# Attention: exponentials multiplied unscaled, inverse row sums applied to a head pair's result

## The chip, the cores and the metric

One core of one Trainium2 chip runs the whole program. Its engines are TensorE (PE, matmuls and transposes), VectorE (DVE), ScalarE (ACT), GpSimd (POOL) and SyncE (SP, which here only issues DMAs). The metric is device time of one execution in microseconds. A profiled execution is a further one, from which the trace comes.

## The reference

Two layers work on x of 512 positions by 1024 channels. Each layer is a gated feed-forward block (FFN), a mixer, and another such block. The mixer projects its normalised input into three branches, two of which are attentions with 8 heads of 64 channels. The change is in these. For each head:

```
logits = q . k + bias            # first attention: by distance; second: by forget gates
logits = where(visible, logits, -1e30)
p = softmax(logits)              # exp(logits - max) / sum
out = p @ v
```

The first attention sees its own chunk of 64 positions and eight chunks before it, the second everything up to the own position. The three branches are multiplied by branch weights, gated, added up and projected back.

## The kernel before, in words

Everything is held transposed: channels on the 128 partitions, the 512 positions (`T`) along the free axis. Matmuls of 32-bit numbers are made of three matmuls of high and low parts (`triple`, lines 117 to 122; `mm` at L119, L120 and L121): each operand is split into `hi`, a rounded copy made by ACT, and `lo`, the rest, made by a subtraction. `split_to` (L377 to L379) does this: ACT copies at L378, DVE or POOL subtracts at L379. Weights come in chunks of 512 KB on SP's queue and are split in `wchunk` (ACT at L271, DVE at L273).

Each attention (`attention`) runs over 8 heads and 4 blocks of 128 query positions (`NT` = 4), so 32 steps, two attentions in each of two layers: 128 steps in all, and 16 pairs of heads. A step has three parts, which are issued at different times:

- `logits`: two matmuls (L951, L952) give the scores of 128 queries against the first `n` = 128 to 512 keys in a PSUM bank. DVE adds the bias strip and takes the maximum (L955), ACT takes the exponential and its row sum (L959), DVE inverts the sum (L961), and the exponentials are multiplied by it (L962), on POOL for the first three blocks of a head and on DVE for the last.
- `turn`: PE transposes the scaled exponentials 128 columns at a time (L974), and ACT and DVE split them into high and low (L978, L979).
- `weigh`: for each half of the queries (two blocks), matmuls of v with the turned exponentials (L996, L997). The head's 64 channels come out in one half of the partitions for v's high part and in the other for its low part; ACT moves one half over (L1000), DVE adds (L1001), and `split_to` splits the sum into the pair's block `y` (ACT at L378, POOL at L379, pieces of 64 partitions by 256 columns).

The order is written by hand: `later(delay, ...)` queues a function until a count of PE work (`pe[0]`, in units of one 512-column matmul) has grown by `delay`, and `poll`, called before each triple, runs what is due. `LAG_T` = 24 is the delay from scores to transposes, `LAG_V` = 14 from there to `weigh`. Between the steps a filler feeds PE: projections for the second attention during the first, gates and the first branch's merge (`merge_units`) during the second, 9.5 and 9.0 units a step. The first merge unit runs all queued work of the first attention (`poll(group="a")`) before it uses the four pair blocks `ys`. From the written order the compiler makes the order on each engine; an engine takes its instructions strictly in that order.

Buffers are rings under a tag, and a tile whose ring is full waits for the oldest to be let go: `t2` has three buffers of 512 columns (exponentials, squares, and others), `t1` two (scores, pieces of the output, gates), `b` 17 blocks of 1024 columns (turned q and k, pair results and others), and four PSUM banks have the tag `mm` (scores, transposes, pieces of the output).

The bias strips of a head are loaded on SP's queue one head ahead; in the first attention POOL clears a corner of them (L926), in the second it masks each with four additions (L937). POOL's queue also copies x to DRAM ahead of a mixer (L1119), and scales half of the blocks of q and k (L839).

Of the kernel before, what the change touches and what calls it, by code (L numbers as in the profile page):

```python
# [15 lines left out]
F32 = mybir.dt.float32  # L16
F32R = mybir.dt.float32r
I32 = mybir.dt.int32
AF = mybir.ActivationFunctionType
ALU = mybir.AluOpType  # L20
AX = mybir.AxisListType

P = 128
T = 512
# [6 lines left out]
HD = 64  # L31
NT = T // P
# [8 lines left out]
def encoder_kernel(tc, xT, c, w_ada, b_ada, gains, w_gate, w_up, w_down, w_qkv, w_f, w_ubg,  # L41
                   qk_gain, rel, fbias, w_pool, pool_scale, w_branch, w_out, inv_cnt, w_first, out):
    nc = tc.nc
    pools = []

    def open_pool(**kw):
        p = tc.tile_pool(**kw)
        pools.append(p)
        return p.__enter__()
# [4 lines left out]
    dr = open_pool(name="dr", bufs=1, space=bass.MemoryType.DRAM)  # L54
# [3 lines left out]
    NB, NRAW = 17, 2  # L58

    def nm(s):  # L60
        uid[0] += 1
        return f"{s}_{uid[0]}"

    def st(shape, dt, tag, bufs):
        return sb.tile(shape, dt, tag=tag, bufs=bufs, name=nm(tag))
# [4 lines left out]
    def mmt(shape=(P, T)):  # L70
        return ps.tile(list(shape), F32, tag="mm", bufs=4, name=nm("mm"))

    def blk(tag, dt=F32R):
        bufs = {"xv": 4, "v2": 4, "b": NB}[tag]
        return st([P, 2, T], dt, tag, bufs)

    def t1(cols=T):
        return st([P, cols], F32, "t1", 2)

    def t2(cols=T):  # L80
        return st([P, cols], F32, "t2", 3)
# [16 lines left out]
    def later(delay, fn, group=None):  # L98
        t = Task(pe[0] + delay, fn, group)
        tasks.append(t)  # L100
        return t

    def poll(everything=False, group=None):
        if polling[0]:
            return
        polling[0] = True
        while True:
            ready = [t for t in tasks if t.fn is None or everything or t.due <= pe[0]
                     or (group is not None and t.group == group)]
            if not ready:  # L110
                break
            t = min(ready, key=lambda z: z.due)
            tasks.remove(t)
            t.run()
        polling[0] = False
# [56 lines left out]

    x_dram = dr.tile([4, P, 2 * T], F32, name="x_dram")
    fv_dram = [dr.tile([H, FVLEN], F32, name=f"fv_dram{l}") for l in range(L)]

    last = {}

# [199 lines left out]
    def split_to(hi, lo, src, lo_eng=nc.vector):  # L377
        nc.scalar.copy(hi, src)  # L378
        lo_eng.tensor_tensor(lo, src, hi.bitcast(F32), op=ALU.subtract)  # L379
# [502 lines left out]
    def finish_turns(upto=3):  # L882

        for todo in turns:
            while len(todo) >= 4 - upto:
                todo.pop(0)()
# [53 lines left out]
    def attention(qs, ks, vs, strip, ys, filler, budget, group):  # L940


        open_pt = {}

        def logits(h, i, strips):
            p, off = divmod(h, 2)
            (q, ql), k = qs[p], ks[p]
            odd = h % 2
            n = (i + 1) * P
            s = mmt()  # L950
            mm(s[:, :n], q[:, odd, i * P:(i + 1) * P], k[:, odd, :n], start=True, stop=False)  # L951
            mm(s[:, :n], ql[:, odd, i * P:(i + 1) * P], k[:, odd, :n], start=False, stop=True)  # L952
            lg = t1(T)[:, :n]
            mx = st([P, 1], F32, "mx", 4)
            nc.vector.tensor_tensor_reduce(out=lg, in0=s[:, :n], in1=strips[i], scale=-1.0, scalar=BIG,  # L955
                                           op0=ALU.add, op1=ALU.min, accum_out=mx)
            pr = t2(T)[:, :n]
            sm = st([P, 1], F32, "sm", 4)
            nc.scalar.activation(pr, lg, AF.Exp, bias=mx, scale=-1.0, accum_out=sm)  # L959
            rs = st([P, 1], F32, "rs", 4)  # L960
            nc.vector.reciprocal(rs, sm)  # L961
            (nc.vector if i == NT - 1 else nc.gpsimd).tensor_scalar(pr, pr, rs, None, op0=ALU.mult)  # L962
            pe[0] += 0.5 * (i + 1.5)
            later(LAG_T, lambda: turn(h, i, pr), group)

        def turn(h, i, pr):
            half, c = divmod(i, 2)
            nj = 2 * half + 2
            if c == 0:
                open_pt[h] = st([P, 2, nj, 256], F32R, "ptb" if half else "pta", 2 if half else 1)  # L970
            pt = open_pt[h]
            tp = mmt()
            for j in range(i + 1):
                nc.tensor.transpose(tp[:, j * P:(j + 1) * P], pr[:, j * P:(j + 1) * P], ident)  # L974
            tv = tp[:, :(i + 1) * P].rearrange("p (j q) -> p j q", q=P)
            dh = pt[:, 0, :i + 1, c * P:(c + 1) * P]
            dl = pt[:, 1, :i + 1, c * P:(c + 1) * P]
            nc.scalar.copy(dh, tv)  # L978
            nc.vector.tensor_tensor(dl, tv, dh.bitcast(F32), op=ALU.subtract)  # L979
            pe[0] += 0.55 * (i + 1)  # L980
            if c == 1:
                later(LAG_V, lambda: weigh(h, half, pt), group)

        def weigh(h, half, pt):
            p, off = divmod(h, 2)
            rows = slice(off * HD, off * HD + HD)
            other = slice(HD - off * HD, 2 * HD - off * HD)
            if off == 0 and half == 0:
                ys.append(blk("b"))
            y = ys[p]  # L990
            o = mmt((P, HALF))
            nj = 2 * half + 2
            for j in range(nj):
                q0 = P if j == nj - 1 else 0
                v2 = vs[j][:, h, :, :].rearrange("p a d -> p (a d)")
                mm(o[:, q0:], v2, pt[:, 0, j, q0:], start=(j == 0), stop=False)  # L996
                mm(o[:, q0:], v2, pt[:, 1, j, q0:], start=False, stop=(j == nj - 1))  # L997
            cols = slice(half * HALF, (half + 1) * HALF)
            yl = t1(T)[:, :HALF]
            nc.scalar.copy(yl[rows, :], o[other, :])  # L1000
            nc.vector.tensor_tensor(yl[rows, :], o[rows, :], yl[rows, :], op=ALU.add)  # L1001
            split_to(y[rows, 0, cols], y[rows, 1, cols], yl[rows, :], nc.gpsimd)
            pe[0] += 1.0 * nj

        for h in range(H):
            strips = strip(h)
            if group == "c":
                finish_turns(h // 2)
            for i in range(NT):
                logits(h, i, strips)  # L1010
                if i == NT - 1:
                    heads[0] = h + 1
                poll()
                goal = pe[0] + budget
                while filler is not None and pe[0] < goal:
                    if next(filler, "end") == "end":
                        filler = None
                poll()
        if filler is not None:
            for _ in filler:  # L1020
                pass

    LAG_T, LAG_V = 24, 14


    def pool_front(l, g):
# [77 lines left out]
    class Mixer:  # L1104
# [10 lines left out]
        def run(self, nxt):  # L1115
# [19 lines left out]

            lo_share[0] = LO_SHARE
            attention(qa, ka, va, lambda h: strip_a(l, h), ya, fill_a(), FILL_A, "a")
            heads[0] = H

# [23 lines left out]
            def fill_c():  # L1163
                yield from merge_units(l, 0, ya, put_a)

            attention(qc, kc, vc, lambda h: strip_c(l, h), yc, fill_c(), FILL_C, "c")
            finish_turns()
            turns.clear()
# [102 lines left out]
```

## Time and profile before

| | |
|---|---|
| median of 3 runs | 2451.54 us |
| lowest and highest run | 2450.65 and 2452.75 us |
| the profiled execution | 2450.88 us |
| its span, first to last instruction | 2448.9 us |
| mean granted clock of TensorE | 0.998 |
| first layer's attentions in the trace | 460 to 690 us |
| second layer's attentions | 1667 to 1895 us |

In the rows of the profile, "line engine operation out<-in xcount" names a group of instructions by the line of the kernel, and tiles by their names in the program with the numbers left off (a tile made by `t1` or `t2` is called `t`). A wait row "A <- B: total, times, longest" says that A stood idle until B had finished. PEld is PE's loading of weights, which runs beside its matmuls. Matmuls overlap, so the duration of one is longer than the distance to the next.

### The profile page before, as it was taken

To read this page: it belongs to the slowest core of one execution; us is meant where nothing else is said; L and a number is where in the kernel's file an instruction comes from. 1 tells how busy PE (TensorE), PEld (TensorE's weight loads), DVE (VectorE), ACT (ScalarE), POOL (GpSimd) and SP (SyncE) were. 2 spreads that over 40 slices of the span, in tenths; PEclk is the share of its full clock that TensorE was granted. 3 is DMA by queue.
4 is the path that set the end of the run, shared out by engine and by line. 5 is a ranking of instruction groups with operands and counts; after the bars stand their busy time and mean duration, and the time that the engine had idled before them with its cause. 6 is when DMAs were issued, how large, how long until landed. Compare 5 with 4: busy or idle time off the path is not lost. (4 is left out here: it accounts for less than half of the span.)

```text
span 2448.9 us, 34028 instructions
## 1 busy us (share of the span) xinstructions
PE 2396.8 (98%) x12966; PEld 2051.8 (84%) x12966; DVE 1600.5 (65%) x2859; ACT 1110.3 (45%) x1888; POOL 377.3 (15%) x439
## 2 busy tenths in 40 slices
PE   7999999999999999999999999999999999999999
PEld 5798888777888898988898888878777888988888
DVE  8978766677643378787678656477765434765463
ACT  5333345677642353333453334366765333533341
POOL 3000002144532110000000000123354322000000
PEclk9999999999999999999999999999999999999999
DMA  7756543222323426565327423223133234233232
GB/s 284 251 170 209 198 147 113 78 82 88 116 91 103 142 75 240 174 206 198 129 85 243 138 86 121 103 90 96 61 109 99 95 111 139 87 104 112 67 114 78
DMA packets 116279, 320.23 MB, mean 131 GB/s; under 512 B 11122, under 2 KB 13298, under 8 KB 116116
## 3 DMA queue, kind: packets, MB, share of 16 engines
q1 hardware_dynamic: 114962, 313.86, 38.3%
q0 software_dynamic: 1152, 4.19, 0.4%
q8 instruction: 102, 1.67, 0.3%
q14 instruction: 61, 0.50, 0.1%
q10 hardware_dynamic: 2, 0.00, 0.0%
HBM read 311.64 MB, written 6.38 MB: 130 GB/s over the span
## 5 line engine op out<-in xcount | busy, mean ns | idle before, releaser
L271 ACT CAST whi<-raw 128x1024 fp32r<-128x1024 f32 (+1 forms) x325 | 338.2, 1044 | 595.1 <-PE mm L120 289.2
L273 DVE TENSOR_TENSOR wlo<-raw,whi 128x1024 fp32r<-128x1024 f32 x317 | 392.2, 1240 | 197.4 <-ACT whi L271 194.2
L121 PE MATMUL mm<-hhi,wlo 128*128 128x512 f32 x744 | 289.8, 390 | 0.7 <-DVE wlo L273 0.4
L119 PE MATMUL mm<-hhi,whi 128*128 128x512 f32 x744 | 290.2, 390 | 0.0
L120 PE MATMUL mm<-hlo,whi 128*128 128x512 f32 x744 | 290.0, 390 | 0.0
L119 PE MATMUL acc<-b,whi 128*128 128x512 f32 (+1 forms) x704 | 264.1, 376 | 1.7 <-ACT b L378 1.7
L121 PE MATMUL acc<-b,wlo 128*128 128x512 f32 (+1 forms) x704 | 262.1, 374 | 3.5 <-DVE wlo L273 3.5
L120 PE MATMUL acc<-b,whi 128*128 128x512 f32 (+1 forms) x704 | 262.4, 373 | 0.0
L197 DVE CUSTOM_DVE_ANT_0 v<-v,b,badac 128x1024 f32<-128x1024 f32 x144 | 188.3, 1316 | 60.9 <-DMA v<-in_w_ada_dram 60.7
L119 PE MATMUL acc<-hhi,whi 128*128 128x512 f32 x480 | 190.7, 399 | 1.7 <-ACT hhi L738 1.7
L121 PE MATMUL acc<-hhi,wlo 128*128 128x512 f32 x480 | 188.9, 394 | 0.0
L120 PE MATMUL acc<-hlo,whi 128*128 128x512 f32 x480 | 188.5, 393 | 0.2 <-DVE hlo L741 0.2
L121 PEld LDWEIGHTS mm<-hhi,wlo 128*128 128x128 f32 x744 | 139.7, 188 | 30.9 <-DVE wlo L273 1.6
L119 PEld LDWEIGHTS mm<-hhi,whi 128*128 128x128 f32 x744 | 140.0, 188 | 27.9
L120 PEld LDWEIGHTS mm<-hlo,whi 128*128 128x128 f32 x744 | 139.7, 188 | 27.4
L121 PEld LDWEIGHTS acc<-b,wlo 128*128 128x128 f32 x704 | 133.8, 190 | 27.2 <-DVE wlo L273 4.6
L119 PEld LDWEIGHTS acc<-b,whi 128*128 128x128 f32 x704 | 133.3, 190 | 23.8 <-ACT b L378 2.6
L120 PEld LDWEIGHTS acc<-b,whi 128*128 128x128 f32 x704 | 133.3, 189 | 23.2 <-DVE b L379 0.9
L119 PE MATMUL acc<-whi,hhi 128*128 128x512 f32 x336 | 137.7, 411 | 4.4 <-ACT t L828 3.7
L120 PE MATMUL mm<-b,whi 128*128 128x512 f32 (+1 forms) x384 | 135.8, 354 | 0.0
L119 PE MATMUL mm<-b,whi 128*128 128x512 f32 (+1 forms) x384 | 135.8, 354 | 0.0
L121 PE MATMUL mm<-b,wlo 128*128 128x512 f32 (+1 forms) x384 | 135.6, 354 | 0.0
(300 smaller groups left out, 5598.3 us busy)
## 6 DMA issues: line engine op xcount, KB each, us to landing
v<-in_w_ada_dram SPq DMA_DIRECT2D x144, 512.0 KB, 4.4
raw<-in_w_down_dram SPq DMA_DIRECT2D x88, 512.0 KB, 3.5
raw<-in_w_up_dram SPq DMA_DIRECT2D x82, 512.0 KB, 3.4
b<-in_w_gate_dram SPq DMA_DIRECT2D x76, 512.0 KB, 5.3
raw<-in_w_ubg_dram SPq DMA_DIRECT2D x56, 512.0 KB, 3.3
raw<-in_w_qkv_dram SPq DMA_DIRECT2D x42, 512.0 KB, 3.7
raw<-in_w_branch_dram SPq DMA_DIRECT2D x24, 512.0 KB, 3.6
raw<-in_w_out_dram SPq DMA_DIRECT2D x16, 512.0 KB, 3.3
```

Of the source, the lines that this page charges most:

```text
L119: mm(o, lh, rh, start=start, stop=False, skip_group_check=onto)
L120: mm(o, lh, rl, start=False, stop=False, skip_group_check=onto)
L121: mm(o, ll, rh, start=False, stop=stop, skip_group_check=onto)
L197: dot = nc.vector.tensor_tensor_reduce(out=raw, in0=raw, in1=silc[0], scale=1.0, scalar=badac[:, l, j, d:d + 1], op0=ALU.mult, op1=ALU.add ...
L271: nc.scalar.copy(hi, raw)
L273: lo_eng.tensor_tensor(lo, raw, hi.bitcast(F32), op=ALU.subtract)
```

## The change

The exponentials are turned and multiplied as they are. The row sums of a pair of heads are collected in one tile of 128 by 8 (partition: query in the block; column: head and block). After the pair's last exponential DVE inverts all of it, and a DMA on POOL's queue writes it to DRAM as two rows of 512. `weigh` adds its pieces into a row block of the `b` ring and no longer splits them. Eight units of PE work after the pair's last piece, `norm_rows` has two DMAs on POOL's queue spread the two rows of inverse sums over 64 partitions each (`rb`, from the `t2` ring); DVE multiplies the whole row block by it, and `split_to` splits it into the pair's block with ACT and DVE.

```diff
+    inv_dram = {(g, p): dr.tile([2, T], F32, name=f"inv_dram_{g}{p}") for g in "ac" for p in range(4)}
...
             pr = t2(T)[:, :n]
-            sm = st([P, 1], F32, "sm", 4)
-            nc.scalar.activation(pr, lg, AF.Exp, bias=mx, scale=-1.0, accum_out=sm)
-            rs = st([P, 1], F32, "rs", 4)
-            nc.vector.reciprocal(rs, sm)
-            (nc.vector if i == NT - 1 else nc.gpsimd).tensor_scalar(pr, pr, rs, None, op0=ALU.mult)
+            if odd == 0 and i == 0:
+                sums[p] = st([P, 2 * NT], F32, "sm", 3)
+            nc.scalar.activation(pr, lg, AF.Exp, bias=mx, scale=-1.0,
+                                 accum_out=sums[p][:, odd * NT + i:odd * NT + i + 1])
+            if odd and i == NT - 1:
+                rs = st([P, 2 * NT], F32, "rs", 2)
+                nc.vector.reciprocal(rs, sums[p])
+                nc.gpsimd.dma_start(inv_dram[group, p].rearrange("h (i q) -> q (h i)", q=P), rs)
             pe[0] += 0.5 * (i + 1.5)
             later(LAG_T, lambda: turn(h, i, pr), group)
...
             if off == 0 and half == 0:
-                ys.append(blk("b"))
-            y = ys[p]
+                rows_of[p] = st([P, T], F32, "b", NB)
+            y = rows_of[p]
...
             nc.scalar.copy(yl[rows, :], o[other, :])
-            nc.vector.tensor_tensor(yl[rows, :], o[rows, :], yl[rows, :], op=ALU.add)
-            split_to(y[rows, 0, cols], y[rows, 1, cols], yl[rows, :], nc.gpsimd)
+            nc.vector.tensor_tensor(y[rows, cols], o[rows, :], yl[rows, :], op=ALU.add)
             pe[0] += 1.0 * nj
+            if off and half:
+                later(LAG_N, lambda: norm_rows(p), group)
+
+        def norm_rows(p):
+            rb = t2(T)
+            for z in range(2):
+                nc.gpsimd.dma_start(rb[z * HD:(z + 1) * HD, :], inv_dram[group, p][z:z + 1, :].broadcast_to([HD, T]))
+            y = blk("b")
+            ys.append(y)
+            full = rows_of[p]
+            nc.vector.tensor_tensor(full, full, rb, op=ALU.mult)
+            split_to(y[:, 0, :], y[:, 1, :], full)
...
-    LAG_T, LAG_V = 24, 14
+    LAG_T, LAG_V, LAG_N = 24, 14, 8
```

More of the change, by code (lines that the diff above doesn't have):

```diff
@@ L943, in attention @@
         open_pt = {}
+        sums, rows_of = {}, {}
         def logits(h, i, strips):
```

## The prediction

> **What bounds the kernel now.** I read the page's first lines, then the busy time by stretch, then the waits of TensorE (PE), and last the groups of instructions that the diff touches.
>
> ```profile
> span 2448.9 us, 34028 instructions
> ## 1 busy us (share of the span) xinstructions
> PE 2396.8 (98%) x12966; PEld 2051.8 (84%) x12966; DVE 1600.5 (65%) x2859; ACT 1110.3 (45%) x1888; POOL 377.3 (15%) x439
> ```
>
> PE is the bound: 98% of the span. Only its idle time can be won, 52 us in all. The next view says where that is; its columns are PE, PEld (weight loads), VectorE (DVE), ScalarE (ACT), GpSimd (POOL), the granted clock and the DMAs.
>
> ```profile
> 460.00:580.00 120.00, 112.20 (x579) 89.03 (x578) 87.99 (x222) 84.93 (x182) 42.53 (x54) 1.00 0.26 80
> 580.00:690.00 110.00, 105.78 (x568) 86.79 (x567) 70.38 (x190) 69.76 (x168) 59.12 (x83) 0.98 0.34 108
> 1667.00:1780.00 113.00, 106.14 (x551) 84.72 (x550) 82.20 (x205) 80.15 (x172) 41.08 (x50) 1.00 0.27 80
> 1780.00:1895.00 115.00, 108.20 (x578) 86.79 (x577) 74.56 (x205) 72.35 (x176) 60.64 (x85) 1.00 0.34 104
> 720.00:860.00 140.00, 140.00 (x622) 116.06 (x621) 51.27 (x53) 43.69 (x56) 29.34 (x17) 1.00 0.36 121
> ```
>
> The first four rows are the two attentions of each layer, the fifth the stretch behind them, where PE never rests. In attention PE is idle for 7.8, 4.2, 6.9 and 6.8 us: 25.7 us is all that this change can reach. DVE and ACT are at 64 to 74% there, so delays on them do get through. The waits of PE from the first attention to the end of the last (total us, times, longest):
>
> ```profile
> PE mm L974 <- POOL t L962: 6.8, 15, 0.7
> PE mm L951 <- DVE t L1001: 4.6, 6, 1.1
> PE mm L951 <- DVE ptb L979: 3.0, 2, 1.5
> ...
> PE mm L951 <- DVE mx L955: 1.8, 4, 0.7
> PE mm L974 <- DVE ptb L979: 1.7, 4, 0.5
> PE mm L997 <- DVE ptb L979: 1.2, 4, 0.3
> PE mm L974 <- DVE rs L961: 1.0, 2, 0.5
> ```
>
> Two rows are transposes (L974) that wait for the scaled exponentials: 6.8 + 1.0 = 7.8 us, the change's own. The other five, 12.3 us, are PE waiting for DVE: scores that want a PSUM bank back, or the low halves of turned weights.
>
> **Part 1: reciprocal and multiply leave each of 128 steps.**
>
> ```profile
> L961 DVE RECIPROCAL rs<-sm x128: 144/162/166, 465.4 to 1887.2; 128x1 f32<-128x1 f32 x128
> L962 POOL TENSOR_SCALAR t<-t,rs x96: 602/927/1253, 465.7 to 1882.5; 128x128 f32<-128x128 f32 x32, 128x256 f32<-128x256 f32 x32, 128x384 f32<-128x384 f32 x32
> L962 DVE TENSOR_SCALAR t<-t,rs x32: 465/487/781, 473.4 to 1887.4; 128x512 f32<-128x512 f32 x32
> ```
>
> Durations are minimum, median and maximum in ns. DVE loses 128 x 0.162 + 32 x 0.487 = 36.3 us of work, POOL 96 x 0.927 = 89 us. The way from exponential to transpose gets shorter by a reciprocal and a multiply, at least 0.144 + 0.465 = 0.6 us, mostly over 1 us. No single wait was longer than 0.7 us, so nearly all of the 7.8 us goes. The same view says who waited for these lines; the weight loads of the transposes stood longer than PE:
>
> ```profile
>   PEld mm L974: 14.0, 20
> ```
>
> The upper bound is that 14.0 plus the 1.0 behind DVE: 15. I take 8, as PE's own rows are the nearer ones. What is late next is the same transpose behind ACT's exponential, or a bank behind DVE: I give back 2 us (bounds 0 and 8).
>
> And it says what DVE itself stood idle for before L961:
>
> ```profile
>   ACT t L959: 37.6, 66
> ```
>
> So DVE stood 37.6 us, 66 times, in front of the reciprocal until ACT had finished the sum. With 16 reciprocals in place of 128, an eighth of it stays: 33 us of blocked queue go. Everything queued behind it (the low halves at L979, L273's subtractions, the score pass L955) moves up. Of PE's 12.3 us behind DVE I take a third, 4 us; bounds 0 and 12.3.
>
> **Part 2: the split moves from 64 quarter pieces to 16 pairs.**
>
> ```profile
> L378 ACT CAST b<-t x64: 388/405/411, 477.1 to 1893.8; 64x256 fp32r<-64x256 f32 x64
> ...
> L378 ACT CAST v<-xv x8: 619/620/620, 782.7 to 2016.4; 128x512 fp32r<-128x512 f32 x8
> ```
>
> ```profile
> L379 POOL TENSOR_TENSOR b<-t,b x64: 723/737/1750, 477.6 to 1894.2; 64x256 fp32r<-64x256 f32 x64
> ...
> L379 DVE TENSOR_TENSOR v<-xv,v x8: 692/693/693, 783.3 to 2017.0; 128x512 fp32r<-128x512 f32 x8
> ```
>
> ACT loses 64 x 0.405 = 25.9 us and gets 16 x 0.620 = 9.9. POOL loses 64 x 0.737 = 47.2. DVE gets, for each pair, one reciprocal, one multiply and one subtraction of 128x512, both priced by the 0.693 row: 16 x (0.162 + 2 x 0.693) = 24.8 us. Against the 36.3 lost, DVE's work falls by 11.5 us in 458 us of attention. That is inside the 4 us above. The buffer `t` of the output piece is free after the add, no longer after POOL's subtraction; ACT and DVE waited for that, PE did not, so it counts as zero.
>
> **Part 3: three DMAs per pair on POOL's queue, and a multiply that waits for them.** No transfer of this shape is in the trace. The nearest are the copy of x to DRAM from POOL's queue, the strips that SyncE's queue (SP) spreads over the partitions from a row of DRAM, and POOL's waits for those:
>
> ```profile
> L1119 POOL DMA_DIRECT2D x_dram<-xv x8: 573/573/762, 365.9 to 1596.4; - x8
> ```
>
> ```profile
> x_dram<-xv POOLq DMA_DIRECT2D x8, 512.0 KB, 3.2
> strip<-in_rel_dram SPq DMA_DIRECT2D x16, 256.0 KB, 2.7
> ssum<-fv_dram SPq DMA_DIRECT2D x16, 256.0 KB, 3.1
> ```
>
> ```profile
> POOL strip L937 <- DMA strip<-fv_dram: 11.9, 11, 2.1
> ```
>
> POOL is busy 0.573 us with issuing a DMA of 128 rows. The two spreading reads have 64 rows each: 2 x 0.573 = 1.15 us, landing 3.1 us later (a row of DRAM spread over partitions, as theirs is). The write has 128 x 8 = 1024 pieces of 4 bytes, because a column of 128 partitions becomes a row in DRAM. Its issue costs between 0.573 us (by DMA) and 8 x 0.573 = 4.6 us (by piece); I take 4.6 since the number of pieces is what differs, and 3.2 us more to land. POOL then has 16 x (4.6 + 1.15) = 92 us more, or 28 at the lower end, against 89 + 47 = 136 us fewer. POOL is no one's bound.
>
> The Trainium skill, page "DMA: Bandwidth & Descriptors", section "Rules for kernel authors", speaks against the write: a DMA whose last dimension is not contiguous becomes one descriptor per element. By that rule the price by piece, 4.6 us, holds and the sum stays as below; its effect here is rival (c); no row here shows such a write.
>
> Who is queued behind: the write waits for the reciprocal, and POOL's queue (clearing and masking of strips, the scaling of q and k) stands behind it. The reads wait for the write and for one of three `t2` buffers, which the exponentials use as well. The multiply waits on DVE for the reads, and L955, L979, L273 stand behind it. Where the compiler puts the multiply in DVE's order decides. POOL's masking shows how well that goes with DRAM reads: 11 waits, 11.9 us, so 1.1 us each. For 16 pairs that is 17 us of DVE standing, half of the 33 us just freed. At the exchange rate of part 1 (4 us of PE for about 44 us of DVE: 33 + 11.5) it costs 2 us; I take 3, as these come in one piece. Bounds: 0, and the second rival.
>
> **Part 4: the hand-over to the merge.** Inside an attention nobody waits for a pair's result; after the first attention the first merge takes all four. From the timeline, the last exponential of the first attention:
>
> ```profile
> 584.20 0.71 ACT L959 ACTIVATE t<-t,mx 128x512 f32<-128x512 f32 x1
> ```
>
> the copy of the last piece:
>
> ```profile
> 594.00 0.36 ACT L1000 COPY t<-mm 64x256 f32<-64x256 f32 x1 [0.98 <-POOL b L379]
> ```
>
> and PE's use of the result:
>
> ```profile
> 596.32 0.40 PE L119 MATMUL acc<-b,whi 128*128 128x512 f32 x1
> ```
>
> New: row sums at about 585, write landed by 585 + 4.6 + 3.2 = 592.8, reads by 592.8 + 1.15 + 3.1 = 597.1, then 0.693 and 0.620 for the high half: 598.4, 2.1 us late. With the cheap write the reads land at 593.1, and the add behind the copy (594.0 + 0.36, and about as long again) is the last, at 594.8: high half at 596.1, in time. Twice in the program, so 0 to 4 us; I take 1, since the copy's own 0.98 us of waiting goes too. After the second attention four pool projections of 24 matmuls each lie between: nothing.
>
> **Sum**, against the profiled execution's 2450.88 us (span 2448.9 and 2.0 around it): -8 + 2 - 4 + 3 + 1 = -6, so 2444.9. The median of the runs, 2451.54, is 0.66 above that execution: **2445.5 us**.
>
> **Rivals.** (a) *Given back in full.* The transposes come on time, but the scores then meet the bank or DVE they would have met anyway. For it: five of seven rows are DVE's, and a queue in order passes time on. Against: DVE is relieved too. Give-back 6, relief 1: -8 + 6 - 1 + 3 + 1 = +1, so 2452 to 2449 with relief 2 to 4; no change.
>
> (b) *DVE stands in front of the multiply.* If the order puts it at the reads' issue, DVE stands up to 1.15 + 3.1 = 4.2 us for each pair. PE's cover is the four PSUM banks: attention has 32 steps in some 114 us, 3.6 us each, and a step takes two banks or more, so cover is under two steps, less DVE's backlog: about 3 us. It decides from 3 us of standing. Beyond it PE loses up to 16 x (4.2 - 3) = 19 us, less the 6 + 3 won elsewhere: +10, 2461. Against: the 1.1 us above.
>
> (c) *The write blocks POOL in front of the masks*, at 4.6 us of issue or more. A head's masks end with
>
> ```profile
> 655.66 0.46 POOL L937 TENSOR_TENSOR ssum<-ssum,cmask 128x128 f32<-128x128 f32 x1
> ```
>
> and are first used at
>
> ```profile
> 657.21 0.28 DVE L955 CUSTOM_DVE_ANT_0 t<-mm,strip 128x128 f32<-128x128 f32 x1
> ```
>
> 656.1 to 657.2 leaves 1.1 us. With 4.6 us of issue in front they are 3.5 late, at three heads of each second attention; (b)'s cover of 3 us leaves 6 x 0.5 = 3. If the issue is twice as dear, 9.2, they are 8.1 late: 6 x 5.1 = 31 us, less the 6 won, 2476. It decides above about 5 us of issue. The rule of the Trainium skill in part 3, one descriptor per element, is what would bring it about. Against: the scaling that stood in POOL's way is gone.
>
> (d) *No shorter.* The row block and its split block want the `b` ring of 17, which holds up to 16 long-lived blocks in attention; the output pieces then wait. About 2450, and 2455 if the next projections wait.
>
> **How the numbers follow.** Forecast 0.50, its own range 2438 to 2449; (a) 0.26, (b) 0.12, (c) 0.07, (d) 0.05. About 0.2%, 4.9 us, is what a measurement can tell from no change. Below 2446.6: 0.44, all from the forecast. Within: the rest of it 0.06, (a) 0.26, half of (d): 0.35. Above 2456.4: (b), (c) and the other half of (d), 0.21. The low end, 2437, is 15 + 12.3 won, half of it given back; the high end, 2459, takes in (a) and most of (b).
>
> **What would show it.** Right: no PE wait on L962; PE idle in the four stretches down from 25.7 to about 20; DVE's work about 11 us lower; waits of DVE for the spread sums near 1 us each; the write's issue on POOL between 0.6 and 4.6 us. Wrong: PE waits at L951 growing by as much as L974's shrank (a); DVE waits of over 3 us on a DMA with PE idle behind (b); DVE waiting for strips (c); PE's busy time itself changed, which nothing here touches.

## The result, and the profile after

| | before | after |
|---|---|---|
| median of 4 runs each, same chip | 2452.14 us | 2533.37 us |
| lowest and highest | 2450.65, 2454.41 | 2527.49, 2533.92 |
| profiled execution | 2450.88 | 2533.92 |

The ratio is 1.0325, with a 95% interval of 1.0307 to 1.0343: the change makes the kernel 81 us slower. The forecast was 6 us faster, and the range ended at 2459. Two executions among the experiments below, of 4.8 and 13.6 ms, were disturbed and are left out of their medians.

In the changed kernel most lines of the attention have moved. The ones needed below: exponential L962, reciprocal L966, the write to DRAM L967, transposes L979, copy and subtraction of turned weights L983 and L984, weighing L1001 and L1002, add of the halves L1006, the two reads L1014, the multiply L1018, the split's copy L379, the strips' load L932 and mask L938.

The page of the changed kernel, its first lines:

```profile
span 2532.2 us, 33690 instructions
## 1 busy us (share of the span) xinstructions
PE 2416.9 (95%) x12966; PEld 2069.8 (82%) x12966; DVE 1590.1 (63%) x2747; ACT 1092.3 (43%) x1840; POOL 256.7 (10%) x327
```

The span grew by 83.3 us. PE's idle time, span less busy, went from 52.1 to 115.3 us (+63.2), and its busy time from 2396.8 to 2416.9 (+20.1) with the same 12966 matmuls. All other engines do less than before: DVE 10.4 us, ACT 18.0, POOL 120.6. So no engine is the new bound; something makes them wait.

Busy time by stretch of the changed kernel, its four attentions (columns as in the prediction):

```profile
460.00:594.00 134.00, 122.49 (x626) 98.94 (x624) 91.07 (x209) 87.93 (x189) 20.23 (x35) 0.97 0.32 85
594.00:738.00 144.00, 112.79 (x563) 93.08 (x560) 62.53 (x147) 58.19 (x140) 21.50 (x45) 0.89 0.32 85
...
1715.00:1850.00 135.00, 123.12 (x633) 99.44 (x631) 92.41 (x212) 89.22 (x193) 20.51 (x35) 0.97 0.35 85
1850.00:1983.00 133.00, 106.80 (x539) 88.21 (x539) 59.37 (x142) 54.85 (x132) 20.22 (x44) 0.91 0.36 87
```

These stretches take 546 us where they took 458. That +88 is not all loss, since they are cut at round times and hold 2361 matmuls where they held 2276. PE's idle time in them says more: it is 80.8 us where it was 25.7, so 55.1 of the 63.2 us more lie here, the most of them in the second attention of each layer (31.2 and 26.2 us idle). The granted clock, 0.98 to 1.00 before, is 0.89 to 0.97.

The longest waits of PE in the changed kernel:

```profile
PE mm L979 <- DVE b L1006: 34.8, 6, 8.8
PE acc L119 <- ACT b L379: 17.7, 4, 8.5
PE acc L119 <- ACT whi L272: 9.8, 4, 3.7
PE mm L1001 <- ACT pta L983: 6.1, 2, 3.2
PE acc L121 <- DVE wlo L274: 5.9, 5, 4.6
```

The wait of the transposes on the scaling is gone, as forecast. In its place stand few, long waits: 34.8 us in 6 pieces for a bank behind DVE, 17.7 us in 4 for a split block. Some of what DVE and POOL wait for, from all waits of the changed kernel:

```profile
POOL strip L938 <- DMA strip<-fv_dram: 143.6, 12, 15.9
...
DVE b L1018 <- DMA t<-inv_dram_c: 75.2, 8, 14.1
```

The masks' wait for the strips was 11.9 us in 11 pieces before, 2.1 at the longest. The strips are not part of the change. But POOL has lost its scaling and is at its masks sooner, so this wait grows even where no strip is late: it is 89.9 us in the kernel with pieces of 32 bytes below, whose strips land in 5.3 us at most and which is faster than the kernel before. The time from a strip's issue to its landing is the plainer sign. For the strips' load, first before (L931), then in the changed kernel (L932):

```profile
DMA to landing us min/median/max: 3.1/3.6/4.3
```

```profile
DMA to landing us min/median/max: 3.1/5.7/12.8
```

And DVE stands up to 14.1 us in front of one multiply.

One chain in full, from the timelines of the changed kernel. POOL issues the write of a pair's inverse sums at 619.63 us. SP, 4 us later, issues the strips of a later head:

```profile
623.81 0.32 SPq L932 DMA_DIRECT2D strip<-fv_dram  x1
```

POOL:

```profile
635.87 1.27 POOL L938 TENSOR_TENSOR strip<-strip,cmask 128x128 f32<-128x128 f32 x3 [13.77 <-DMA strip<-fv_dram]
637.08 1.05 POOL L1014 DMA_DIRECT2D t<-inv_dram_c  x2
```

DVE:

```profile
629.30 0.56 DVE L984 TENSOR_TENSOR ptb<-mm,ptb 128x384 fp32r<-128x384 f32 x1
640.67 0.69 DVE L1018 TENSOR_TENSOR b<-b,t 128x512 f32<-128x512 f32 x1 [10.81 <-DMA t<-inv_dram_c]
```

The strips, issued at 623.81, land at 635.87: 12 us, where the median is 5.7 in this kernel's issues and 3.6 before. POOL has stood in front of its masks for 13.77 us. The reads of the inverse sums are queued behind the masks on POOL and go out at 637.08. DVE has stood in front of the multiply since 629.86 (629.30 + 0.56) and gets on at 640.67. Everything DVE owes PE stands behind it.

What the DMAs did meanwhile, in the same stretch of the changed kernel (last three columns: granted clock, busy share of the DMA engines, GB/s):

```profile
598.00:602.00 4.00, 3.83 (x29) 3.37 (x28) 3.21 (x11) 2.40 (x7) 0.00 (x0) 1.00 0.11 12
602.00:606.00 4.00, 3.78 (x22) 2.70 (x20) 1.32 (x5) 2.45 (x8) 0.00 (x0) 1.00 0.15 16
606.00:609.00 3.00, 0.38 (x2) 0.00 (x0) 0.00 (x0) 0.00 (x0) 0.41 (x1) 0.92 0.99 306
609.00:613.00 4.00, 0.00 (x0) 0.00 (x0) 0.00 (x0) 0.00 (x0) 3.59 (x9) 0.50 0.57 204
613.00:616.00 3.00, 1.27 (x3) 1.08 (x4) 1.99 (x5) 1.52 (x4) 0.00 (x0) 0.50 0.00 0
...
619.00:622.00 3.00, 3.00 (x17) 2.53 (x17) 2.55 (x6) 2.87 (x8) 2.35 (x2) 1.00 0.22 24
622.00:627.00 5.00, 5.00 (x30) 4.20 (x29) 3.25 (x10) 2.56 (x8) 0.10 (x1) 1.00 0.11 27
627.00:632.00 5.00, 5.00 (x29) 4.26 (x28) 2.16 (x6) 3.08 (x8) 0.00 (x0) 1.00 0.29 31
632.00:636.00 4.00, 2.40 (x13) 1.75 (x11) 0.00 (x0) 0.00 (x0) 0.13 (x1) 1.00 0.85 274
```

From 619 to 632 us, behind the write at 619.63, the core's DMAs move 24 to 31 GB/s, and then, at once, 274. Behind the write before, issued at 593.44, it is 12 and 16, and then 306. SP had issued strips and chunks of weights in both stretches, so transfers were waiting, and something let them go. The write itself, by its line:

```profile
L967 POOL DMA_DIRECT2D inv_dram_c<-rs x8: 915/916/924, 619.6 to 1963.0; - x8
...
DMA to landing us min/median/max: 9.2/10.8/12.4
```

Its issue costs POOL 0.92 us, its landing 10.8 us: for 4 KB.

### The profile page after: what moved, and what is told of

It reads as the page before. It is cut to its first block, busy times and chain, and to the rows that moved or that the text cites. A ratio compares the mean times of both kernels' runs of the same rounds, so it can differ in the third digit from the quotient of the medians.

```text
span 2532.2 us, 33690 instructions
## 1 busy us (share of the span) xinstructions
PE 2416.9 (95%) x12966; PEld 2069.8 (82%) x12966; DVE 1590.1 (63%) x2747; ACT 1092.3 (43%) x1840; POOL 256.7 (10%) x327
## 4 chain that ended last, share of the span: by engine, by line
PE 75%; DMA 10%; DVE 7%; ACT 4%; issue 2%; POOL 1%; SPq 0%; POOLq 0%; DVEq 0%; ACTq 0%
PE acc L119 15%; PE acc L121 15%; PE acc L120 15%; PE mm L119 9%; PE mm L120 9%; PE mm L121 9%; DMA strip<-fv_dram 3%; DMA v<-in_w_ada_dram 2%; DVE v L198 1%; DMA t<-inv_dram_c 1%; DMA raw<-in_w_qkv_dram 1%; DVE wlo L274 1%; DMA t<-inv_dram_a 1%; ACT whi L272 1%; DMA inv_dram_c<-rs 1%
## 5 line engine op out<-in xcount | busy, mean ns | idle before, releaser
L119 PE MATMUL acc<-b,whi 128*128 128x512 f32 (+1 forms) x704 | 264.5, 377 | 17.7 <-ACT b L379 17.7
L119 PE MATMUL acc<-hhi,whi 128*128 128x512 f32 x480 | 197.0, 412 | 11.5 <-ACT whi L272 9.8
```

Source lines behind the costliest of these rows:

```text
L119: mm(o, lh, rh, start=start, stop=False, skip_group_check=onto)
```

## The experiments

**Two theories.** Theory 1: the write, 1024 pieces of 4 bytes laid side by side in DRAM, holds up all other transfers of the core for the 10 us until it has landed; strips and weights come late, whoever reads the row. Theory 2: the DMAs as such do no harm; it is the queues, the reads behind the masks on POOL and the multiply behind the reads on DVE, that pass on one slow landing.

**The write alone.** The kernel before, scaling and all, with the 16 writes added; nobody reads what they write. PE, DVE and ACT run the instructions of the kernel before in the same order.

```
+                inverse[p] = st([P, 2 * NT], F32, "rs", 3)
...
+            if odd and i == NT - 1:
+                nc.gpsimd.dma_start(inv_dram[group, p].rearrange("h (i q) -> q (h i)", q=P), inverse[p])
```

> The kernel before, with one thing added: the inverse sums of a pair are also collected in a tile of 128 by 8 and written to DRAM in 4-byte pieces; nobody reads them, the multiply by step stays. Theory 1 (the write itself holds up every other transfer for about 10 us, as 29 GB/s in 622 to 632 us against 334 GB/s right behind it shows): weights and strips land late 16 times and the time rises to 2480 to 2530, with PE waiting for DMA-fed engines. Theory 2 (the loss comes from the queues: reads behind POOL's masks, the multiply in front of DVE's queue): nobody waits for this write, 2450 to 2458.

2507.52 us in one run, 55.8 above the 2451.74 of the kernel before on that chip. From its waits, and the landing of its write:

```profile
POOL strip L938 <- DMA strip<-fv_dram: 50.3, 12, 8.6
```

```profile
DMA to landing us min/median/max: 9.3/10.6/12.0
```

Nobody reads what this write leaves, and POOL still has its scaling, yet the strips' wait is four times the 11.9 us of before; strips land up to 11.2 us after their issue where it was 4.3. Theory 2 alone falls: without its reads and its multiply 56 us are lost, and it is transfers that come late.

**The rest without the write.** The changed kernel with the write taken out; the rows that the reads fetch are filled with ones once, at the start, so the result is not scaled by the sums.

```
+            for v in inv_dram.values():
+                nc.sync.dma_start(v.rearrange("h (i q) -> (h i) q", q=P), ones[:2 * NT, :])
...
-                nc.gpsimd.dma_start(inv_dram[group, p].rearrange("h (i q) -> q (h i)", q=P), rs)
```

> The changed kernel without the 16 writes: the DRAM rows are filled with ones once at the start, so the result stays unscaled by the sums; reads, multiply and split stay. Theory 1: 2440 to 2458, about the kernel before. Theory 2: the reads still stand behind POOL's masks and the multiply still in front of DVE's queue, so most of the 81 us stays: 2490 to 2530.

2441.87 us in one run, 9.9 below the kernel before. Reads, multiply, split and hand-over together do not eat the gain.

**The same number of bytes in pieces of 32.** Each partition writes its 8 sums side by side, 128 pieces. The order of instructions on PE, DVE, ACT and POOL is that of the changed kernel; what the reads fetch comes in another order, so rows are scaled by the wrong sums.

```
-    inv_dram = {(g, p): dr.tile([2, T], F32, name=f"inv_dram_{g}{p}") for g in "ac" for p in range(4)}
+    inv_dram = {(g, p): dr.tile([P, 2 * NT], F32, name=f"inv_dram_{g}{p}") for g in "ac" for p in range(4)}
-                nc.gpsimd.dma_start(inv_dram[group, p].rearrange("h (i q) -> q (h i)", q=P), rs)
+                nc.gpsimd.dma_start(inv_dram[group, p], rs)
...
-                nc.gpsimd.dma_start(rb[z * HD:(z + 1) * HD, :], inv_dram[group, p][z:z + 1, :].broadcast_to([HD, T]))
+                nc.gpsimd.dma_start(rb[z * HD:(z + 1) * HD, :], inv_dram[group, p].rearrange("(z a) c -> z (a c)", z=2)[z:z + 1, :].broadcast_to([HD, T]))
```

> The changed kernel, with the write in the order of the tile: 128 pieces of 32 bytes in place of 1024 of 4, the same 4 KB. The rows that come back are in another order, so a result row is scaled by the wrong sum. The order on PE, DVE and ACT is the same as in the changed kernel. Theory 1 (cost by piece): the landing falls from 9 to 12 us to 2 to 4, the time to 2440 to 2460. Theory 2: POOL waits for the write either way, over 2500.

2439.65 us (2438.52 to 2440.67), ratio 0.9953 [0.9938, 0.9968], 12.1 us faster than before. Waits of POOL and DVE in this kernel, and the landing of its write:

```profile
POOL strip L938 <- DMA strip<-fv_dram: 89.9, 12, 13.2
...
DVE b L1018 <- DMA t<-inv_dram_c: 24.1, 7, 5.2
DVE b L1018 <- DMA t<-inv_dram_a: 4.8, 5, 1.3
```

```profile
DMA to landing us min/median/max: 1.7/2.1/4.0
```

Only the pieces of the write and the order of what is read differ from the changed kernel, and 93 us go (81.2 + 12.1). PE is idle for 18.7 us in the four attentions, and DVE stands 28.9 us in front of 16 multiplies, 1.8 each.

**Which property of the write?** Three kernels, all with the write alone as in the first experiment. Half the pieces, 512, still 4 bytes apart:

```
+                nc.gpsimd.dma_start(inv_dram[group, p][0:1, :].rearrange("h (i q) -> q (h i)", q=P), inverse[p][:, :NT])
```

> As the run with the write alone, but only the row of the even head is written: 512 pieces of 4 bytes in place of 1024. If the cost goes by piece (about 10 us by 1024), the landing is 5 to 6.5 us and the time about half of the way from the kernel before to the write alone: 2470 to 2485. If it is a fixed cost of a write with a scattered row, the landing stays at 9 to 12 us and the time at 2495 to 2515.

All pieces, but issued by SP:

```
+                nc.sync.dma_start(inv_dram[group, p].rearrange("h (i q) -> q (h i)", q=P), inverse[p])
```

> As the run with the write alone, but issued from SP's queue, whose descriptors hardware makes, and not from POOL's. If the cost lies in what POOL does for such a DMA, landing falls to 2 to 4 us and the time to 2450 to 2470 (SP waits a little for the reciprocals). If it lies with the 1024 pieces at the memory, landing stays at 9 to 12 us and the time is 2495 to 2525.

All 1024 pieces from POOL, but each in 64 bytes of its own:

```
+    inv_dram = {(g, p): dr.tile([2, T, 16], F32, name=f"inv_dram_{g}{p}") for g in "ac" for p in range(4)}
...
+                nc.gpsimd.dma_start(inv_dram[group, p].rearrange("h (i q) w -> q (h i) w", q=P)[:, :, 0], inverse[p])
```

> As the run with the write alone, but every piece of 4 bytes goes to its own 64 bytes of DRAM (rows 16 times as long). If pieces that share a short stretch of DRAM wait for each other, the landing falls to 2 to 5 us and the time to 2450 to 2475. If the cost goes by piece wherever it lies, 9 to 12 us and 2495 to 2520.

The kernel before beside them ran 2450.49 us (median of six), these one run each. Half the pieces: 2496.44, +46.0. From SP: 2496.93, +46.4. In 64 bytes each: 2450.71, +0.2. The landings of the write, in that order:

```profile
DMA to landing us min/median/max: 8.7/9.7/10.8
```

```profile
DMA to landing us min/median/max: 9.0/10.4/11.3
```

```profile
DMA to landing us min/median/max: 2.9/3.2/6.0
```

Half the pieces save a tenth of the landing: it is not a price by piece. From SP's queue the landing is the same: it is not POOL's queue. Both cost about 9 us less than the +55.8 of the first run, which was taken on another chip; what makes up the 9 stays open. The same 1024 pieces from the same queue, spread out, land in 3.2 us and cost nothing that one run can show: it is that pieces as small as 4 bytes lie side by side (those of 32 bytes do so too, and land in 2.1 us).

**How far apart is enough?** The same with the last size 8, 4 and 2, that is 32, 16 and 8 bytes from piece to piece.

> The same with pieces 32 bytes apart, two to 64 bytes. Theory 3: landing 3.2 to 4.2 us, 2450 to 2460; if the stretch is 32 bytes long, as at 64 bytes, 3.2 us. Theory 4: 9 to 12 us, 2490 to 2515.

> As the run with the write alone, with the 1024 pieces of 4 bytes 16 bytes apart, so 4 share 64 bytes where 16 did. Theory 3 (pieces that share one short stretch of DRAM wait for each other, the stretches side by side; 512 pieces at the same spacing took as long as 1024): 16 pieces cost 10.7 us to land and one 3.2, so 4 should land in about 3.2 + 3 x 0.5 = 4.7 us; the time 2455 to 2475. Theory 4 (only whole 64-byte neighbours are free, any sharing costs all): 9 to 12 us and 2490 to 2515.

> As the run with the write alone, with the 1024 pieces 8 bytes apart, so 8 share 64 bytes. Landing was 3.2 us with one piece to 64 bytes, 3.3 with two, 3.7 with four and 10.7 with sixteen. If the wait grows with the neighbours step by step, eight land in 5 to 8 us and the time is 2460 to 2485. If there is a step between four and sixteen, it is either 3.7 to 4.5 us and 2450 to 2458, or 9.5 to 11.5 us and 2490 to 2512.

One run each: 2454.25 (+3.9), 2453.38 (+3.0) and 2456.74 (+5.5; the kernel before ran 2450.37 beside the first two, 2451.21 beside the last). Landing at 8 bytes:

```profile
DMA to landing us min/median/max: 3.8/4.4/6.8
```

The medians are 3.3, 3.7 and 4.4 us, so with 64 bytes and the dense write: 3.2, 3.3, 3.7, 4.4, then 10.6. A slow slope and a step between 8 and 4 bytes. Theory 4 of the expectations falls, and so does the even price for each neighbour in theory 3: it had 4.7 us at 16 bytes. The differences of 3 to 5.5 us are little above the scatter of single runs (2448.99 to 2451.94 for the kernel before).

**How much hangs on the queues?** The changed kernel with its dense write, the reads on SP's queue:

```
-                nc.gpsimd.dma_start(rb[z * HD:(z + 1) * HD, :], inv_dram[group, p][z:z + 1, :].broadcast_to([HD, T]))
+                nc.sync.dma_start(rb[z * HD:(z + 1) * HD, :], inv_dram[group, p][z:z + 1, :].broadcast_to([HD, T]))
```

> The changed kernel as it is, scattered write included, with the two spreading reads on SP's queue. The write alone costs 56 us of the change's 81. If the other 25 us come from reads that stand on POOL behind masks whose strips are late, the time falls to 2495 to 2512. If they come from DVE waiting for reads that the slow stretch of DMA itself delays, it stays at 2520 to 2535.

2500.36 us in one run, 50.0 above the 2450.37 of the kernel before. Its waits:

```profile
POOL strip L938 <- DMA strip<-fv_dram: 132.0, 13, 16.2
...
DVE b L1018 <- DMA t<-inv_dram_c: 44.6, 8, 9.2
```

The strips still come late (they land in 7.1 us in the median and in up to 11.9), but the reads no longer stand behind the masks, and the multiply's longest wait falls from 14.1 to 9.2 us. So 31 of the 81 us (81.2 - 50.0) hang on the reads' place: theory 2 has its share, on top of theory 1. With the reads the compiler also moved a few instructions of DVE and ACT, such as score passes ahead of a step of the first branch's merge (L1161) in three places of each layer; how much of the 31 us is theirs was not tried. What is left, 50, is about the write alone and the rest without it: 55.8 - 9.9 = 45.9.

**A version with the right result and no harmful write.** PE turns the 128x8 inverse sums, ACT copies them out of PSUM, and 8 rows of 512 bytes go to DRAM, 30 units of the planner behind the last scores.

```
-                nc.gpsimd.dma_start(inv_dram[group, p].rearrange("h (i q) -> q (h i)", q=P), rs)
+                later(LAG_S, lambda: write_sums(p, rs), group)
...
+        def write_sums(p, rs):
+            tp = mmt((P, P))
+            nc.tensor.transpose(tp[:2 * NT, :], rs, ident)
+            rt = st([P, P], F32, "rt", 1)
+            nc.scalar.copy(rt[:2 * NT, :], tp[:2 * NT, :])
+            nc.gpsimd.dma_start(inv_dram[group, p].rearrange("h (i q) -> (h i) q", q=P), rt[:2 * NT, :])
```

> A version with the right result and no scattered write: PE turns the 128 by 8 inverse sums, ACT copies them, and 8 pieces of 512 bytes go to DRAM 30 units after the last scores. Theory 1: landing 2 to 4 us, no slow stretch of DMA, 2440 to 2462; 16 small transposes and copies cost PE under 5 us. Theory 2: over 2490, as reads and multiply stand where they stood.

2449.21 us (2446.54 to 2452.40), ratio 0.9988 [0.9978, 0.9997]: 2.5 us faster than before. The write lands in 2.1 us, but the row is written later than in the experiment with 32-byte pieces, and the reads still stand on POOL (the multiply is L1025 here, the low halves of turned weights L991, the add L1013):

```profile
PE mm L953 <- DVE ptb L991: 10.1, 4, 4.7
...
DVE b L1025 <- DMA t<-inv_dram_c: 15.7, 5, 4.3
DVE b L1025 <- DMA t<-inv_dram_a: 10.3, 6, 2.9
```

DVE's wait for the reads, 26.0 us, is no longer than the 28.9 of the kernel with 32-byte pieces, so it is not what makes this version 9.6 us slower than that one. PE's wait for the low halves is longer, 10.1 us in place of 2.1; why, no run shows.

**The same with the reads on SP's queue.**

```
-                nc.gpsimd.dma_start(rb[z * HD:(z + 1) * HD, :], inv_dram[group, p][z:z + 1, :].broadcast_to([HD, T]))
+                nc.sync.dma_start(rb[z * HD:(z + 1) * HD, :], inv_dram[group, p][z:z + 1, :].broadcast_to([HD, T]))
```

> The version in which PE turns the inverse sums, with the spreading reads on SP's queue, where no mask of a strip stands ahead of them. If the wait of DVE for the reads comes from POOL's queue, it falls from 26 us to under 13, and the time from 2449 to 2438 to 2446. If it comes from the transfer itself or SP's queue holds the reads as long, 2446 to 2454.

2433.90 us (2432.36 to 2434.83), ratio 0.9934 [0.9912, 0.9955]: 16.6 us faster than the kernel before, 98 faster than the changed one (81.2 + 16.6). Its page and its waits of DVE:

```profile
PE 2390.2 (98%) x12982; PEld 2052.9 (84%) x12982; DVE 1590.7 (65%) x2747; ACT 1094.8 (45%) x1856; POOL 236.5 (10%) x295
```

```profile
DVE b L1025 <- DMA t<-inv_dram_c: 9.4, 8, 3.6
DVE b L1025 <- DMA t<-inv_dram_a: 4.3, 4, 1.3
```

DVE stands 13.7 us in front of the multiplies where it stood 26.0, and PE is idle for 40.4 us of 2430.6, against 52.1 before. Moving two small reads to a queue without the masks is worth 14 us (16.6 - 2.5) even with a write that does no harm. Here too a few instructions of DVE and ACT changed places with them.

**One step further.** The write issued by ACT, and the reads and the multiply 16 units behind the last weighing in place of 8.

```
-    LAG_T, LAG_V, LAG_N = 24, 14, 8
+    LAG_T, LAG_V, LAG_N, LAG_S = 24, 14, 16, 30
...
+            nc.scalar.dma_start(inv_dram[group, p].rearrange("h (i q) -> (h i) q", q=P), rt[:2 * NT, :])
```

> The version in which PE turns the sums and SP reads, with the write on ACT's queue right behind ACT's copy, and the multiply 16 units behind the last piece in place of 8. If the 14 us that DVE still waits for the reads count, 2428 to 2434; if nothing waits behind them, 2432 to 2437; the handing-over to the first merge comes later, which could cost up to 4.

2440.05 us (2439.24 to 2441.50), ratio 0.9958 [0.9942, 0.9975]: 10.3 us faster than before, but 6 less than the version above, and DVE's waits for the reads are 15.3 us, not fewer. PE waits more behind DVE:

```profile
PE mm L953 <- DVE b L1013: 7.4, 6, 1.6
PE acc L121 <- DVE wlo L274: 6.3, 3, 3.5
```

The first was 4.3, the second 3.8 in the version above. A later multiply did not find its row any earlier. Two things were changed at once, so which of them costs the 6 us stays open.

## Why the prediction was wrong, step by step

**Part 1 held for the transposes, not for the rest.** The waits of the transposes on the scaling (7.8 us) are gone; 0.4 us behind the exponential came back. DVE stands 6.0 us in front of the reciprocal where it stood 37.6. Without a harmful write the change gives 9.9, 12.1, 2.5, 16.6 and 10.3 us in the five kernels above, where the sum had 6. But that the total is met is in part luck. The trace of the kernel with 32-byte pieces, which has the changed kernel's order of instructions, is 10.0 us shorter than before: 4.3 us are PE's idle time and 5.7 its busy time, which the sum held fixed. PE's waits behind DVE, from which part 1 took 4 us, are 17.6 us there from the first attention to the end of the last, and 16.3 before. One of them is new, transposes that wait for a bank:

```profile
PE mm L979 <- DVE b L1006: 4.6, 5, 2.2
```

With the reads on SP's queue they are 11.0. What made the busy time shorter stays open.

**Part 2 held.** DVE 10.4 us less (forecast 11.5), ACT 18.0 (16). POOL is relieved by 120.6 us; the forecast had 136 less 92, mostly since it took the write's issue at 4.6 us in place of 0.92.

**Part 3 is the step that failed**, in the words "I take 4.6 since the number of pieces is what differs, and 3.2 us more to land". Both halves looked for the price of 1024 pieces on POOL's queue. It is not there: the issue is 0.92 us. It is in the landing, 10.8 us in place of 3.2, and above all in what the landing does to transfers that the step never listed: 24 to 31 GB/s for the whole core in the stretch shown, with sixteen such writes, all landing in 9.2 us or more. The 3.2 us came from the copy of x, 128 rows of 4 KB, a row that has the same queue and nothing else in common with pieces of 4 bytes. The sentence "its effect here is rival (c)" bounded the unknown at POOL's queue and left out the transfers of SP's queue, which had the cost. The write alone shows it: +55.8 us, though nothing waits for what it writes.

The same part's "1.1 us each" for the multiply's waits was near the mark without the dense write (28.9 us for 16 is 1.8, and 13.7 is 0.9 with the reads on SP's queue), and is 6.2 us with it: 75.2 + 24.7 for 16.

**Part 4** had the hand-over at 0 to 2.1 us each. The wait of the merge for the split block is 17.7 us in 4, up to 8.5; with 32-byte pieces it is 1.8 us in 2. So the size fits a write that lands fast, which this one does not. Two figures of the working are a touch off, with no term hanging on them: its rows give 63 to 73% for DVE and ACT, not 64 to 74, and 593.0 for the reads behind a cheap write, not 593.1.

**The rivals.** (a) is seen in part, in the new wait of the transposes for banks in part 1; (d) was not tried. (b) names the mechanism that passes much of the loss to PE, DVE standing in front of the multiply, but with a bound of 4.2 us per pair, worked out from the same landing; measured are up to 14.1. (c) looked at the right DMA and found the wrong price. The Trainium skill's rule there ("DMA: Bandwidth & Descriptors", "Rules for kernel authors"), one descriptor per element where the last dimension is not contiguous, warns of this write rightly. But by that rule the write in 64-byte places has as many descriptors, and it cost 0.2 us: the count is not what is paid for. The Trainium skill's table on the same page ("DMA: Bandwidth & Descriptors", "Specifications") says that below 512 bytes a transfer is done as read-modify-write. All the writes of 4 bytes are below it, 8 bytes apart (4.4 us) as well as 4 bytes apart (10.6), and so is the one of 32-byte pieces (2.1): the threshold does not tell them apart. That neighbours in one small block of DRAM have to be done one after another would fit the step between 8 and 4 bytes; no run here shows it, and why other transfers stand meanwhile stays open too.

**"PE's busy time itself changed, which nothing here touches"** was listed as what would prove the prediction wrong, and it did change, by 20.1 us. The rows by stretch beside the DMAs, in the result, show the clock: 0.50 at 609 to 616, 1.00 from 619. PE's own rows there, from the timeline of the changed kernel:

```profile
606.00 0.39 PE L121 MATMUL acc<-hhi,wlo 128*128 128x512 f32 x1
614.73 1.22 PE L119 MATMUL acc<-b,whi 128*128 128x512 f32 x2 [8.34 <-ACT b L379]
615.75 0.63 PE L119 MATMUL acc<-hhi,whi 128*128 128x512 f32 x1
```

PE stops at 606.39 and stands for 8.34 us behind the split block. A matmul of the same size that took 0.39 us takes 0.63 after it. Cut finer, to 1 us, the clock says when it fell and when it rose:

```profile
608.00:609.00 1.00, 0.00 (x0) 0.00 (x0) 0.00 (x0) 0.00 (x0) 0.41 (x1) 0.77 1.05 408
...
618.00:619.00 1.00, 1.00 (x6) 1.00 (x6) 0.56 (x1) 1.00 (x4) 0.00 (x0) 0.61 0.50 172
```

A mean of 0.77 between 1 and 0.5 is a fall at 608.5, 2.1 us after PE stopped; 0.61 is a rise at 618.8, 4.1 us after it started again. In the next stall, from 634.39 to 642.34, the same reading gives 4.9 us and 3.7. The Trainium skill ("TensorE: Matmul & The Clock Gate", "What's actually happening") has half the clock after an idle window of about 3.4 us and the full one after as long of work, in a window that runs freely. The trace agrees in kind; the fall 2.1 us after PE stopped is sooner than a whole idle window would have it.

Over whole kernels PE's busy time goes roughly with its idle time: 40.4 us idle and 2390.2 busy (turned by PE, read by SP), 52.1 and 2396.8 (before), 115.3 and 2416.9 (after). The stretches at half clock, added up over the trace, are 85.4 us in the changed kernel, with 57.7 us of PE's work in them, and 11.8 us with 8.7 before. If that work took twice its time, 28.8 and 4.4 us of it are the clock's: an estimate of 24 us more, enough for the 20.1. No run changes the clock by itself.

## What to carry to other kernels

Price a DMA by its smallest piece in DRAM and by what lies next to it, and ask what it does to every other transfer in flight, not only who waits for it: for the sums of a column, let PE turn them first, so that whole rows go to DRAM. Put a read that an engine will stand and wait for on a queue where what stands ahead of it does not wait for late data itself; here that was worth 14 us, and 31 beside the slow write. A stall of PE is dearer than its length: count the slow clock after it.

## What the runs showed of the hardware that was not expected

- 4 KB written as pieces of 4 bytes side by side land in 10.6 us, and in the two stretches shown the core's other DMAs move 12 to 31 GB/s meanwhile (274 and 306 right behind). The same pieces 8, 16, 32 and 64 bytes apart land in 4.4, 3.7, 3.3 and 3.2 us, half as many side by side in 9.7.
- Their landing is the same from SP's queue as from POOL's (10.4 us), and their issue is cheap: 0.92 to 0.96 us on POOL for 1024 pieces, 0.82 for 512, 0.37 to 0.43 on SP for 1024.
- In the busy share of the DMA engines the hold-up looks like rest: 0.11 to 0.29 while transfers wait. Only the burst behind it, and a landing three times as long as that of spread pieces, give it away.
- PE's clock was at half 2.1 us after PE had stopped in one stall and 4.9 us in the next, and full again 4.1 and 3.7 us after it had started.
